# Earlier output norms and spills on another queue in a one-layer hybrid decoder kernel

## The chip, the cores and the metric

The kernel runs on one core of one Trainium2 chip. A core has TensorE (PE, the matrix multiplier; its weight loads are shown as PEld), VectorE (DVE), ScalarE (ACT), GpSimd (POOL) and SyncE (SP, which here only issues DMAs). Each engine works through its own list of instructions in order and waits for the others by semaphores. The metric is the device time of one execution in microseconds (us); lower is better.

## The reference, cut to what matters

One layer of a decoder for 256 prompt tokens and 8 sample tokens (264 in all). The parts that the change touches are the two mixers and the projection behind them:

```python
z = rmsnorm(x, g_mix) @ w_in
# recurrence ("rg"): gated linear recurrence over the prompt
h_rg, h_last = rglru(conv(z_rgx), r, i, lam, h0)
y_rg = rmsnorm(h_rg * gelu(z_rgg), g_rg_out)             # 1024 wide
# matrix memory ("ml"): 4 heads, q and k 128 wide, v 256 wide
num, den, C_new, n_new, m_new = mlstm(q, k, v, logi, logf, C0, n0, m0)
h_ml = rmsnorm(num / den, g_ml_out)                      # per head
y_ml = h_ml * sigmoid(z_o)
x = x + concat([y_rg, y_ml]) @ w_out
```

Behind them come cross attention over 256 memory tokens (w_q, w_k, w_v, w_o) and a gated feed-forward part. Outputs are the activations and the new states, the sample tokens' state matrices (o_sc, 4 heads of 8 tokens) among them.

## The kernel before, in words

**Tiling.** Activations lie transposed: 128 features on the partitions, 264 tokens along the free axis. The weights are worked off as a list `steps` of blocks of 2048 rows by 128 columns. A step is 16 chunks of 128 rows, and each chunk is three matmuls of 264 columns in fp32r (`mm3`: high by high, high by low, low by high, into one PSUM bank), so a step is 48 matmuls `mm<-B,W`. Steps 17 to 24 make v, 25 to 32 the recurrence's gate, 33 to 40 the output gate o, 41 to 56 w_out, and so on.

**Weights.** `load_piece` has SP load each block as two raw halves of 512 KB into 5 buffers, three steps ahead (a load waits until its buffer's old half has been split). `split_half`, a step ahead of use, has ACT copy a half to its high part and DVE subtract for the low part; `st["low"]` is that last subtraction.

**Side work.** Everything else is written as generators that are advanced between steps (`pump`); `yield STEP` puts the rest off to the next step. Small jobs that PE does in the middle of a step go through `later(job, after=k)`: jobs stand in one list, and after each chunk the first one's count falls by one, until at zero it is placed (`drip`); `finish` places everything at once. A step's evacuation (scaling the PSUM bank and so on) is kept in `pend` and written at the start of the next step, but not in steps 4, 5, 34 and 35 (L1439), so that the evacuations of steps 33, 34 and 35 are written at the start of step 36. SP's list is in the program's order; the other engines' lists are ordered by a scheduler within the program's dependences and priorities.

**The recurrence's output norm.** `rg_out` (L588) copies and subtracts the sum of squares `acc_rg` into two parts, waits a step, reduces over the partitions by two matmuls with `ones_r`, makes 1/sqrt by three Newton rounds on rows of 264 (`rstd_wide`, L384), and then scales each of the 8 blocks `h` and splits it in two (`split`) as `yrg`, which steps 41 onwards read chunk by chunk.

**The matrix memory.** For each head, `ml_heads` multiplies the masked weights with v, and writes k times its weights (`kw`) and, for every second head, v to DRAM (`kspill`, 128 KB a head, L774; `vspill`, 516 KB for two heads, L776); they are read back in the last 12 steps. The sample tokens' states are fetched by POOL: `B<-c0T` (L842, 512 KB) and two broadcast reads `B<-scr` (L846, 256 KB each) per half head, a half head ahead; ACT forms products `t<-B,B` from them, DVE updates the state, and POOL writes it out (`o_sc`, L870). POOL issues the spills in the same list. V's evacuation in that stage is `B<-ax 128x512` on ACT, which PE waits for with the head's product matmuls `ax<-B,B`.

**The matrix memory's norm.** `ml_norm` (L874) sums squares over partitions with `token_sums` (three matmuls `ax<-ones,B` a head, four heads), makes a factor `f` of 12 columns (4 heads by 3 windows of tokens) with a Newton chain on [128,12], spreads it over the partitions (`spread`, three fp32 matmuls a head: f's column, broadcast, against the identity), and multiplies `hh` by it. `evac_o` needs a head's scaled `hh`.

Of the kernel before, what the change touches and what calls it, by code (L numbers as in the profile page):

```python
# [10 lines left out]
F32 = mybir.dt.float32  # L11
F32R = mybir.dt.float32r
# [12 lines left out]
H = 4  # L25
# [65 lines left out]
def layer_kernel(ctx: ExitStack, tc, xT, memT, vec, wrg, w_in, w_out, w_q, w_k, w_v, w_o,  # L91
# [26 lines left out]
    def B(shape, dt=F32, skip=0):  # L118
        return view(sb.tile([P, SLOT], dt, tag="B", bufs=NB, name=nm("B")), shape, skip)
# [51 lines left out]
    steps = []  # L171
    LD, LS = 3, 1
    GATES = 8

    raws, splits = {}, {}

# [105 lines left out]
    def later(*fs, after=0):  # L282
        k = [after, list(fs)]
        drips.append(k)
        return k
# [13 lines left out]
    def bank(tag="mm"):  # L299
        return psm.tile([P, 512], F32, tag=tag, bufs=4, name=nm(tag))  # L300
# [58 lines left out]
    def spread(ps, c, n=N):  # L359

        for j in range(2 if n == T else 3):
            lo, hi = (j * P, j * P + P) if j < 2 else (T, N)
            i = pe.matmul(ps[:, lo:hi], c[j].to_broadcast([P, P]), ident[:, P - (hi - lo):], start=True, stop=True)
        return i
# [19 lines left out]
    def rstd_wide(acc, y, n):  # L384

        w = acc.shape[-1]
        hl, vt = B([P, 2, w], F32R), B([P, 3, w])
        act.activation(hl[:, 0], acc, AF.Copy)
        dve.tensor_sub(hl[:, 1], acc, hl[:, 0].bitcast(F32))
        yield STEP  # L390
        ps = bank("ax")
        for k in range(2):
            pe.matmul(ps[:, :w], ones_r, hl[:, k], start=k == 0, stop=k == 1)
        v, i, t = vt[:, 0], vt[:, 1].bitcast(I32), vt[:, 2]
        dve.tensor_scalar(v, ps[:, :w], 1.0 / n, EPS, op0=OP.mult, op1=OP.add)
        dve.tensor_single_scalar(i, v.bitcast(I32), 1, op=OP.logical_shift_right)
        dve.tensor_scalar(y.bitcast(I32), i, -1.0, 1597463007.0, op0=OP.mult, op1=OP.add)
        for _ in range(3):
            dve.tensor_mul(t, y, y)
            dve.scalar_tensor_tensor(t, t, -0.5, v, op0=OP.mult, op1=OP.mult)  # L400
            dve.scalar_tensor_tensor(y, t, 1.5, y, op0=OP.add, op1=OP.mult)
        yield 0.1

    def sumsq(acc, x, first):
        if first:
# [180 lines left out]
        return f  # L586

    def rg_out():  # L588
        yield STEP
        rr = ltmp()  # L590
        yield from rstd_wide(acc_rg, rr, RGB * P)
        st["yrg"] = HL(RGB)
        for n in range(RGB):
            h = rg["h"](n)
            dve.tensor_mul(h, h, rr)
            split(*st["yrg"](n), h, V("g_rg", n))
            yield 0.75

# [158 lines left out]
    def ml_heads():  # L757
        hT["t"] = Arr(8)
        hh = hT["t"]
        one = ones[:, 0:1]  # L760
        for h in range(H):
            while min(ml.get("pn", 0), ml.get("vtn", 0)) <= h:
                yield STEP
            while st["i"] < ml["pi", h] + 3:
                yield STEP
            vt = ml["vt", h]
            Pm, kw, p2 = ml["w", h]
            nps = bank("ax")
            for vb in range(2):
                o = vb * T  # L770
                pe.matmul(nps[:, o: o + T], vt[:, 0, vb * P: vb * P + P], Pm[:, 0:256], start=True, stop=False)
                pe.matmul(nps[:, o + P: o + T], vt[:, 1, vb * P: vb * P + P], Pm[:, 256:384],
                          start=False, stop=True)
            pool_e.dma_start(kspill[:, h, :], kw)  # L774
            if h % 2:
                pool_e.dma_start(vspill[h // 2], ml["vts"][h // 2].rearrange("p t h v -> p (t h v)"))  # L776
            dps = bank("ax")[:, 0:2]
            pe.matmul(dps[:, 0:1], Pm[:, 0:P], one, start=True, stop=True)
            pe.matmul(dps[:, 1:2], p2, one, start=True, stop=True)
            for vb in range(2):  # L780
                act.activation(hh(2 * h + vb)[:, 0:T], nps[:, vb * T: vb * T + T], AF.Copy)
            act.activation(den[:, 3 * h: 3 * h + 2], dps, AF.Abs)
        yield STEP
# [89 lines left out]
    def ml_norm():  # L873
# [15 lines left out]
        def sums(h):  # L889
# [10 lines left out]
                dve.tensor_mul(f, f, r)  # L900
            return i

        for h in range(H):
            k = later(lambda h=h: sums(h), after=3 if h else 1)
        while k[1]:
            yield STEP
        for h in range(H):
            ps = bank("ax")
            spread(ps, [f[:, 3 * h + j: 3 * h + j + 1] for j in range(3)])
            for vb in range(2):  # L910
                dve.tensor_mul(hh(2 * h + vb), hh(2 * h + vb), ps[:, :N])
            yield 0.7
            ml["nn"] = h + 1

    def evac_o(j):
        def f(ps):
# [512 lines left out]
    for i, (src, cols, pef, evf, need) in enumerate(steps):  # L1429
# [6 lines left out]
            if q in st:  # L1436
                finish(lambda: st[q].done)
        st["i"] = i
        if i not in (4, 5, 34, 35):  # L1439
            with tc.high_priority(300):  # L1440
                for e, x in pend:
                    e(x)
            pend = []
# [4 lines left out]
        if i + LS < len(steps) and steps[i + LS][1] > 1024:  # L1448
            split_half(i + LS, 1, parts)
        ps = pef(i)  # L1450
        if 1 <= i < 4:
            with tc.issue_after(st["split"].ins):
                for q in ((0, 1), (2,), (3,))[i - 1]:
                    square(q)
# [132 lines left out]
```

## Time and profile before

| quantity | value |
|---|---|
| time, median of 3 runs | 1537.24 us (1536.81 to 1538.69) |
| the profiled execution's own time | 1538.44 us |
| its span, first to last instruction | 1536.4 us (so 2.0 us lie around it) |
| granted TensorE clock, mean | 0.998 |
| busy: PE, DVE, ACT, POOL | 99%, 69%, 51%, 8% of the span |
| DMA rate over the span | 214 GB/s, 329 MB |

Times in the profile are in us from the span's start. A row of a timeline gives start, length, engine, line, operation, output<-input and the number of instructions put together; in square brackets stands idle time before it and what ended it. Nearly all instructions are recorded through one helper and so carry line L63; the names of tiles tell them apart. "L63 PE MATMUL mm<-B,W" is a weight matmul; "ax" is a PSUM bank of side work. Lengths of pipelined matmuls overlap, so the pitch from start to start is what counts. Some matmul records can be missing.

### The profile page before, as it was taken

How to read it: one execution, taken by the hardware profiler on the slowest of the kernel's cores; microseconds unless marked ns; L12 is line 12 of the kernel's file. 1: busy time of each engine (PE TensorE's matmuls, PEld its weight loads, DVE VectorE, ACT ScalarE, POOL GpSimd, SP SyncE). 2: the span in 40 equal slices, each digit the busy share in tenths (PEclk: the TensorE clock that was granted, in tenths of full speed). 3: DMA queues.
4: the chain of work that ended last, by engine and by line, in shares of the span. 5: the costliest groups of instructions: out<-in, count | busy, mean ns of one | idle time of the engine just before them, and what ended most of it. 6: DMA issues, size and time to landing. Idle time of an engine off the chain costs nothing.

```text
span 1536.4 us, 30014 instructions
## 1 busy us (share of the span) xinstructions
PE 1525.2 (99%) x12038; PEld 1490.6 (97%) x12038; DVE 1059.4 (69%) x2012; ACT 782.8 (51%) x1233; POOL 129.7 (8%) x195
## 2 busy tenths in 40 slices
PE   9999999999999999999999999999999999999997
PEld 9999999999998888899999999999999999999997
DVE  7976898878898989966665555455555544555554
ACT  7555784655555666654544444334444433344463
POOL 0001220000233434400000000000000000000000
PEclk9999999999999999999999999999999999999999
DMA  8646896556798798755555555555555555555573
GB/s 297 206 154 203 302 320 234 180 183 238 258 339 333 242 343 326 250 163 191 182 187 180 183 189 179 186 184 180 188 182 181 189 180 185 186 180 186 158 226 119
DMA packets 93659, 329.17 MB, mean 214 GB/s; under 512 B 10992, under 2 KB 11936, under 8 KB 93520
## 3 DMA queue, kind: packets, MB, share of 16 engines
q1 hardware_dynamic: 77904, 273.03, 53.1%
q0 software_dynamic: 15472, 54.22, 9.9%
q8 instruction: 94, 1.54, 0.4%
q14 instruction: 45, 0.37, 0.1%
q10 hardware_dynamic: 144, 0.01, 0.0%
HBM read 314.36 MB, written 12.86 MB: 213 GB/s over the span
## 4 chain that ended last, share of the span: by engine, by line
PE 95%; DMA 2%; ACT 1%; DVE 1%; issue 0%; POOL 0%; DVEq 0%; POOLq 0%
PE mm L63 91%; PE ax L63 4%; DMA B<-scr 1%; DMA xres<-xT 1%; DVE B L63 1%; DMA raw<-w_in 0%; ACT B L63 0%; DMA scr<-lt 0%; DMA vecs<-vec 0%; ACT t L63 0%; DVE W L63 0%; ACT L63 0%; ACT W L63 0%; POOL kspill L774 0%; DVE t L63 0%
## 5 line engine op out<-in xcount | busy, mean ns | idle before, releaser
L63 PE MATMUL mm<-B,W 128*128 128x264 f32 (+2 forms) x11008 | 1363.3, 285 | 0.6 <-DVE W L63 0.4
L63 PEld LDWEIGHTS mm<-B,W 128*128 128x128 f32 x11008 | 1340.5, 188 | 12.7 <-DVE W L63 0.6
L63 ACT ACTIVATE W<-raw 128x1024 fp32r<-128x1024 f32 (+2 forms) x520 | 536.6, 1034 | 637.3 <-PE mm L63 436.6
L63 DVE TENSOR_TENSOR W<-raw,W 128x1024 fp32r<-128x1024 f32 (+2 forms) x520 | 620.1, 1195 | 347.6 <-ACT W L63 346.4
L63 PE MATMUL mm<-W,B 128*128 128x512 f32 x384 | 92.4, 395 | 0.0
L63 PEld LDWEIGHTS mm<-W,B 128*128 128x128 f32 x384 | 70.9, 188 | 16.1
L1479 POOL TENSOR_TENSOR B<-B,rstd 128x264 f32<-128x264 f32 x4 | 2.8, 734 | 854.1 <-ACT rstd L63 854.1
L63 DVE TENSOR_TENSOR t<-mm,rstd 128x264 f32<-128x264 f32 x104 | 44.8, 432 | 43.5 <-PE mm L63 43.3
L63 DVE TENSOR_TENSOR xres<-xres,mm 128x264 f32<-128x264 f32 (+1 forms) x81 | 34.3, 425 | 34.5 <-PE mm L63 34.4
L63 DVE SCALAR_TENSOR_TENSOR B<-B,dw 128x256 f32<-128x256 f32 x128 | 53.9, 476 | 1.8 <-ACT dw L63 1.7
L63 DVE SCALAR_TENSOR_TENSOR dw<-B,qsm,dw 128x256 f32<-128x256 f32 x96 | 50.8, 538 | 1.9 <-ACT dw L63 1.6
L1115 POOL TENSOR_TENSOR dr<-dw,dr 128x256 fp32r<-128x256 f32 x32 | 38.5, 1205 | 102.6 <-ACT dr L63 102.5
L63 PE MATMUL ax<-B,B 128*128 128x256 f32 (+2 forms) x272 | 44.7, 303 | 1.0 <-ACT B L63 1.0
L63 PEld LDWEIGHTS ax<-B,B 128*128 128x128 f32 x272 | 38.4, 190 | 3.5 <-ACT B L63 1.2
L63 ACT ACTIVATE B<-xres,vecs 128x264 fp32r<-128x264 f32 (+1 forms) x64 | 31.0, 502 | 2.2 <-DMA xres<-xT 2.1
L1104 POOL DMA_DIRECT2D B<-kcT x32 | 17.4, 543 | 134.8 <-DVE B L63 126.5
L63 ACT ACTIVATE t<-t 128x264 f32<-128x264 f32 (+1 forms) x61 | 24.7, 407 | 4.5 <-DVE t L63 4.5
L63 ACT ACTIVATE dw<-B,qsm 128x256 f32<-128x256 f32 x32 | 16.3, 508 | 20.7 <-DVE B L63 9.2
L63 ACT ACTIVATE B<-t 128x264 fp32r<-128x264 f32 (+1 forms) x60 | 24.5, 408 | 4.4 <-DVE t L63 4.4
L63 ACT ACTIVATE t<-B,B 128x128 f32<-128x128 f32 x64 | 20.2, 388 | 12.1 <-DMA B<-scr 12.1
L63 ACT ACTIVATE t<-xres 128x264 f32<-128x264 f32 (+2 forms) x46 | 18.8, 410 | 14.6 <-DVE xres L63 14.6
L63 DVE SCALAR_TENSOR_TENSOR B<-xres,vecs,B 128x264 fp32r<-128x264 f32 x48 | 22.4, 490 | 1.1 <-ACT B L63 1.1
(168 smaller groups left out, 659.0 us busy)
## 6 DMA issues: line engine op xcount, KB each, us to landing
raw<-w_gu SPq DMA_DIRECT2D x176, 512.0 KB, 3.6
raw<-w_d SPq DMA_DIRECT2D x80, 512.0 KB, 3.6
raw<-w_in SPq DMA_DIRECT2D x78, 512.0 KB, 5.1
raw<-w_out SPq DMA_DIRECT2D x32, 512.0 KB, 3.6
raw<-w_q SPq DMA_DIRECT2D x32, 512.0 KB, 5.6
B<-kcT POOLq DMA_DIRECT2D x32, 512.0 KB, 8.0
B<-vcT POOLq DMA_DIRECT2D x32, 512.0 KB, 8.9
raw<-w_k SPq DMA_DIRECT2D x32, 512.0 KB, 6.3
```

What stands on the lines that cost most here:

```text
L63: return f(*a, **k)
L1104: pool_e.dma_start(kc, kcT[h, b])
L1115: pool_e.tensor_sub(wr[:, 1], acc, wr[:, 0].bitcast(F32))
L1479: e.tensor_mul(st["y"](c), st["y"](c), r)
```

## The change

Three things, each by moving or replacing instructions:

1. **Recurrence's output norm.** The wait of a step before the reduction is gone; its two matmuls are placed by `later(..., after=15)`. The scalings of the 8 blocks are tied to steps (`RGAT`) and to come behind that step's last weight subtraction.
2. **Matrix memory's norm.** The sums of the four heads follow each other by one chunk instead of three. The factor f (12 columns) is turned into rows once (`turn`: three fp32 matmuls with 4-column weights, output 4 rows of 264), split into high and low rows, and spread by two one-pass fp32r matmuls a head against a 4-row selector (`scale`), in place of three fp32 matmuls a head. The evacuations of steps 33 to 35 are now written at the end of step 36's code.
3. **Spills.** `kspill` and `vspill` are issued from SP's list instead of POOL's.

```diff
+    RGAT = (37, 37, 37, 38, 38, 38, 39, 39)
 def rstd_wide(acc, y, n):
-            pe.matmul(ps[:, :w], ones_r, hl[:, k], start=k == 0, stop=k == 1)
+            last = pe.matmul(ps[:, :w], ones_r, hl[:, k], start=k == 0, stop=k == 1)
...
-        yield 0.1
+        yield last
 def rg_out():
-        yield STEP
         rr = ltmp()
-        yield from rstd_wide(acc_rg, rr, RGB * P)
+        wide = rstd_wide(acc_rg, rr, RGB * P)
+        next(wide)
+        k = later(lambda: next(wide), after=15)
+        while k[1]:
+            yield STEP
         st["yrg"] = HL(RGB)
         for n in range(RGB):
+            while st["i"] < RGAT[n]:
+                yield STEP
             h = rg["h"](n)
-            dve.tensor_mul(h, h, rr)
+            with tc.issue_after(st["low"].ins):
+                dve.tensor_mul(h, h, rr)
             split(*st["yrg"](n), h, V("g_rg", n))
 def ml_heads():
-            pool_e.dma_start(kspill[:, h, :], kw)
+            sp.dma_start(kspill[:, h, :], kw)
             if h % 2:
-                pool_e.dma_start(vspill[h // 2], ml["vts"][h // 2].rearrange("p t h v -> p (t h v)"))
+                sp.dma_start(vspill[h // 2], ml["vts"][h // 2].rearrange("p t h v -> p (t h v)"))
 def ml_norm():
+        fp = bank("ax")
+        hl = B([P, 2, N], F32R)[0:4]
+        def turn():
+            fj = f.rearrange("p (h j) -> p j h", j=3)
+            for j, w0 in enumerate((0, P, T)):
+                w = min(P, N - w0)
+                i = pe.matmul(fp[0:4, w0: w0 + w], fj[:, j, :], ident[:, P - w:], start=True, stop=True)
+            act.activation(hl[:, 0], fp[0:4, :N], AF.Copy)
+            dve.tensor_sub(hl[:, 1], fp[0:4, :N], hl[:, 0].bitcast(F32))
+            return i
+        def scale(h):
+            ps = bank("ax")
+            sel = ident_r[:, h: h + 1].to_broadcast([4, P])
+            for k in range(2):
+                i = pe.matmul(ps[:, :N], sel, hl[:, k], start=k == 0, stop=k == 1)
+            with tc.issue_after(st["low"].ins):
+                for vb in range(2):
+                    dve.tensor_mul(hh(2 * h + vb), hh(2 * h + vb), ps[:, :N])
+            ml["nn"] = h + 1
+            return i
         for h in range(H):
-            k = later(lambda h=h: sums(h), after=3 if h else 1)
+            later(lambda h=h: sums(h), after=1)
+        for h in range(H):
+            if h == 0:
+                later(turn, after=19)
+            k = later(lambda h=h: scale(h), after=1 if h else 6)
         while k[1]:
             yield STEP
-        for h in range(H):
-            ps = bank("ax")
-            spread(ps, [f[:, 3 * h + j: 3 * h + j + 1] for j in range(3)])
-            for vb in range(2):
-                dve.tensor_mul(hh(2 * h + vb), hh(2 * h + vb), ps[:, :N])
-            yield 0.7
-            ml["nn"] = h + 1
 # the loop over the steps
-        if i not in (4, 5, 34, 35):
+        if i not in (4, 5, 34, 35, 36):
...
         ps = pef(i)
+        if i == 36:
+            with tc.high_priority(300):
+                for e, x in pend:
+                    e(x)
+            pend = []
```

What this does to the engines' lists shows in three places. Numbers behind a tile's name count the tiles; an `x2` is two equal instructions in a row.

**POOL's and SP's lists in steps 23 to 32.** POOL before, from the second half head's reads to the fourth's state: the spills stand between the state's writes and the next fetches.

```order
L846 DMA B_1957<-scr 128x512 x2
L776 DMA vspill<-B_1541 128x1032
L870 DMA o_sc<-B_1874 128x1024
L774 DMA kspill<-B_1862 128x256
L842 DMA B_2068<-c0T 128x1024
L846 DMA B_2069<-scr 128x512 x2
L870 DMA o_sc<-B_1956 128x1024
L774 DMA kspill<-B_1955 128x256
L774 DMA kspill<-B_2054 128x256
L774 DMA kspill<-B_2154 128x256
L842 DMA B_2262<-c0T 128x1024
```

POOL after, the same stretch:

```order
L853 DMA B_1957<-scr 128x512 x2
L877 DMA o_sc<-B_1874 128x1024
L849 DMA B_2068<-c0T 128x1024
L853 DMA B_2069<-scr 128x512 x2
L877 DMA o_sc<-B_1956 128x1024
L849 DMA B_2262<-c0T 128x1024
```

SP after, from the second load for step 29 to the first for step 32 (before, the same weight loads stand there with nothing between them):

```order
L188 DMA raw_2341<-w_in 128x1024
L781 DMA kspill<-B_1955 128x256
L783 DMA vspill<-B_1541 128x1032
L188 DMA raw_2448<-w_in 128x1024
L188 DMA raw_2450<-w_in 128x1024
L781 DMA kspill<-B_2054 128x256
L188 DMA raw_2557<-w_in 128x1024
L188 DMA raw_2559<-w_in 128x1024
L781 DMA kspill<-B_2154 128x256
L783 DMA vspill<-B_1542 128x1032
L188 DMA raw_2666<-w_in 128x1024
```

The six spills have left POOL, so that the fetch of B_2068 and B_2069 stands right behind the first state's write; on SP the first spill (not among these rows) stands behind the loads for step 28, and the last two stand between the loads for step 31 and those for step 32.

**ACT's list in step 24.** B_2069 holds what `scr` gives, W_2083 is the high part of half a weight block for step 25, and B_1542 is v, evacuated, for which PE waits. Before:

```order
L63 ACTIVATE B_1955<-B_1619,B_1955 128x128
L63 ACTIVATE W_2083<-raw_1938 128x8x128
L63 ACTIVATE t_2267<-B_2069,B_1545 128x128
L63 ACTIVATE B_1542<-ax_2055 128x2x256
L63 ACTIVATE t_2267<-B_2069,B_1545 128x128
L63 ACTIVATE t_2273<-B_2069,B_1545 128x128 x2
L63 ACTIVATE B_2054<-B_2054 128x384
```

After:

```order
L63 ACTIVATE B_1955<-B_1619,B_1955 128x128
L63 ACTIVATE t_2267<-B_2069,B_1545 128x128 x2
L63 ACTIVATE t_2273<-B_2069,B_1545 128x128 x2
L63 ACTIVATE W_2083<-raw_1938 128x8x128
L63 ACTIVATE B_1542<-ax_2055 128x2x256
L63 ACTIVATE B_2054<-B_2054 128x384
```

All four products from B_2069 now stand ahead of the weight copy and of v's evacuation; before, one of them did.

**PE's list around step 37.** c_3089 and c_3109 are the factor f, B_3111 its rows in two parts, mm_3326 (before) and mm_3318 (after) the bank of step 37, mm_3208 (after) that of step 36. Before, the spreads stand five matmuls into step 37:

```order
L63 MATMUL mm_3326<-B_144,W_3244 128x264 x2
L63 MATMUL mm_3326<-B_145,W_3244 128x264
L63 MATMUL ax_3185<-ident,c_3089 128x128 x2
L63 MATMUL ax_3185<-ident,c_3089 128x8
L63 MATMUL ax_3191<-ident,c_3089 128x128 x2
L63 MATMUL ax_3191<-ident,c_3089 128x8
L63 MATMUL ax_3197<-ident,c_3089 128x128 x2
L63 MATMUL ax_3197<-ident,c_3089 128x8
L63 MATMUL ax_3203<-ident,c_3089 128x128 x2
L63 MATMUL ax_3203<-ident,c_3089 128x8
L63 MATMUL mm_3326<-B_144,W_3244 128x264 x2
```

After, the turn stands three quarters into step 36, and the selector matmuls between steps 36 and 37:

```order
L63 MATMUL mm_3208<-B_173,W_3115 128x264
L63 MATMUL ax_3110<-ident,c_3109 4x128 x2
L63 MATMUL ax_3110<-ident,c_3109 4x8
L63 MATMUL mm_3208<-B_183,W_3115 128x264
L63 MATMUL mm_3208<-B_184,W_3115 128x264
```

```order
L63 MATMUL mm_3208<-B_183,W_3115 128x264
L63 MATMUL ax_3265<-B_3111,ident_r 128x264
L63 MATMUL ax_3270<-B_3111,ident_r 128x264
L63 MATMUL ax_3275<-B_3111,ident_r 128x264
L63 MATMUL ax_3280<-B_3111,ident_r 128x264
L63 MATMUL ax_3275<-B_3111,ident_r 128x264
L63 MATMUL ax_3270<-B_3111,ident_r 128x264
L63 MATMUL ax_3265<-B_3111,ident_r 128x264
L63 MATMUL ax_3280<-B_3111,ident_r 128x264
L63 MATMUL mm_3318<-B_144,W_3202 128x264
```

Twelve fp32 matmuls are replaced by three fp32 and eight fp32r ones. The two `ax<-B,ones_r` matmuls of the recurrence's norm, which stood in the middle of step 37, stand after the last matmul of step 34.

## The prediction

> **What bounds the kernel now.** I read the page first: busy shares, clock, and the chain of work that ended last.
>
> ```profile
> PE 1525.2 (99%) x12038; PEld 1490.6 (97%) x12038; DVE 1059.4 (69%) x2012; ACT 782.8 (51%) x1233; POOL 129.7 (8%) x195
> PE 95%; DMA 2%; ACT 1%; DVE 1%; issue 0%; POOL 0%; DVEq 0%; POOLq 0%
> ```
>
> TensorE is busy for 99% of the span and makes 95% of the chain; its granted clock is 0.998, so it isn't slowed. Time can then go in two ways only: PE has fewer or shorter instructions, or one of its waits goes. What the waits hold in all is the next view, PE's waits by releaser (us in total, times, longest):
>
> ```profile
> PE ax L63 <- ACT B L63: 1.5, 2, 1.0
> PE mm L63 <- DVE ones L63: 1.1, 1, 1.1
> PE mm L63 <- DVE W L63: 0.4, 1, 0.4
> PE mm L63 <- ACT W L63: 0.2, 1, 0.2
> ```
>
> About 3.2 us, of which 1.1 is the start (`ones`). So the waits that a reordering could take away are worth about 2 us. The third view gives the price of PE's work: the groups of PE by form (busy us, mean ns).
>
> ```profile
> L63 PE MATMUL mm<-B,W 128*128 128x264 f32 x10496 | 1269.9, 282 | 0.6 <-DVE W L63 0.4 <-ACT W L63 0.2
> L63 PE MATMUL ax<-ident,c 128*128 128x128 f32 x32 | 5.2, 288 | 0.0
> L63 PE MATMUL ax<-B,ident_r 4*128 4x256 f32 x8 | 2.0, 328 | 0.0
> ```
>
> 1269.9 us over 10,496 weight matmuls are 0.121 us each (the 282 ns are latency, which overlaps). A step of 48 is 5.8 us. Now PE's timeline where the norms lie (start, length, count):
>
> ```profile
> 234.69 0.72 PE L63 MATMUL ax<-ones,B 128*128 128x1 f32 x6
> ...
> 241.63 7.30 PE L63 MATMUL mm<-B,W 128*128 128x264 f32 x59
> 248.77 2.74 PE L63 MATMUL ax<-ident,c 128*128 128x128 f32 x24
> 251.37 2.55 PE L63 MATMUL mm<-B,W 128*128 128x264 f32 x19
> 253.75 0.41 PE L63 MATMUL ax<-B,ones_r 128*128 128x264 f32 x2
> 254.00 22.07 PE L63 MATMUL mm<-B,W 128*128 128x264 f32 x183
> 276.50 8.72 PE L63 MATMUL mm<-B,W 128*128 128x264 f32 x70 [0.43 <-DVE W L63]
> ```
>
> The reader sees the first of four sums, the spread of the matrix memory's factor (24 passes, since each fp32 matmul is two), the reduction of the recurrence's norm, and one wait 0.43 long at 276, in step 41. It is booked to a weight split, but the recurrence's scaled blocks are what comes last there:
>
> ```profile
> 273.61 1.70 DVE L63 SCALAR_TENSOR_TENSOR B<-B,vecs,B 128x264 fp32r<-128x264 f32 x4
> 275.23 1.22 DVE L63 TENSOR_TENSOR W<-raw,W 128x1024 fp32r<-128x1024 f32 x1
> 276.36 0.89 DVE L63 SCALAR_TENSOR_TENSOR B<-B,vecs,B 128x264 fp32r<-128x264 f32 x2
> ```
>
> DVE makes the low parts of `yrg` (B<-B,vecs,B) until 275.2, and a weight subtraction then ends about when PE goes on; step 41 is where `yrg` is read first.
>
> **The change, part by part.**
>
> *The matrix memory's spread.* Removed: the 24 passes, which hold PE from 248.77 to 251.37, 2.60 us; the 19 weight matmuls behind them take 2.38 to the next group, 0.10 over their 19 at 0.120, which goes with them. Saved 2.70. Added, `turn`: a quarter of that work with 4-column weights. Its price isn't in the trace; a quarter of 2.60 is 0.65, with the way back 0.75; 0.70 is taken. Added, `scale`: eight one-pass matmuls of 264 columns whose weights have 4 rows. The nearest rows are the pairs against `ident_r` with 4 rows, ahead of step 24:
>
> ```profile
> 159.24 0.50 PE L63 MATMUL ax<-B,ident_r 4*128 4x256 f32 x2
> 159.67 0.92 PE L63 MATMUL ax<-B,B 128*128 128x256 f32 x4
> 160.43 0.60 PE L63 MATMUL ax<-ident,B 128*128 128x128 f32 x4
> ```
>
> The pair takes 0.43 to the next group, where two at 0.117 (256 of 264 columns at 0.121) would take 0.23: 0.20 over for entering. The four behind take 0.76 for 0.47: up to 0.29 over for leaving, though part of that is the next group's own change of form. Eight in a row enter and leave once: 8 x 0.121 = 0.97, plus 0.20 to 0.49; 0.35 is taken, so 1.32. The Trainium skill, "TensorE: Matmul & The Clock Gate", section "Why this matters for your kernels", says that a single matmul with K = 32 takes as long as one with K = 128; by it these eight cost 0.97 and the whole sum would be 2.7 saved instead of 2.3. The rows above show more than that, and the rows decide. The four sums only move (one chunk apart instead of three), so PE's count there stays. In all: -2.70 + 0.70 + 1.32 = **-0.68**, with ends at -0.5 and -1.1.
>
> What this could bring instead: the chain of sums, Newton, turn, ACT copy, DVE subtraction, selectors must be done in time. The sums stand earlier and closer than before; of the Newton chain the trace shows the end.
>
> ```profile
> 245.94 0.17 DVE L63 TENSOR_TENSOR c<-c,c 128x12 f32<-128x12 f32 x1
> ```
>
> f is done at 246.1 now, from a last sum that ends at 241.6. Of the 59 matmuls from 241.63 the last 53 are step 36 and five of step 37, so step 36 begins at 248.77 - 53 x 0.121 = 242.4, and PE reaches the turn 36 matmuls later, at 246.7: 0.6 to spare even if the chain ended no sooner than now, and its last sum is earlier. The copy and the subtraction behind the turn (an estimate of 0.43 each, from DVE's 1.70 for four operations of 264 columns above) have the 12 matmuls that follow it, 1.4 us. Behind the selectors only the weights of step 37 are queued, and for the scaled `hh` waits only `evac_o`, on DVE and ACT. I cost this at nothing; if f is late, PE stands still until it is there, up to 0.5 us.
>
> *The recurrence's norm.* Reduction and Newton rounds move ahead by more than two steps, and the scalings to steps 37 to 39, so that a whole step of 5.8 us lies between the last of them and step 41's reads. That is the room that DVE's other work there may use up. The `ones_r` pair costs the same 0.25 (253.75 to 254.00) elsewhere. They stand at the start of step 35, six matmuls (0.7) ahead of the first sum at 234.69, so at 234.0, and need DVE's subtraction from `acc_rg`:
>
> ```profile
> 233.34 0.43 DVE L63 TENSOR_TENSOR B<-acc_rg,B 128x264 fp32r<-128x264 f32 x1
> ```
>
> It ends at 233.8: tight, by 0.2. The wait at 276 goes. Its worth: 254.00 to 276.50 is 22.50 us for 183 matmuls, 0.54 over 183 at 0.120, while records can be missing from the row (then less); the listed idle time is 0.43, and the next matmul is longer too. I take **-0.60**, bounds 0.43 and 0.75. What is late next there: the weight split ending at 276.4, if it doesn't move up with DVE's freed time; three of the recurrence's operations stood ahead of it, so it does.
>
> *The spills.* The second large wait on PE is at the start of step 25:
>
> ```profile
> 166.71 0.50 PE L63 MATMUL ax<-B,ident_r 4*128 4x256 f32 x2
> 168.20 0.92 PE L63 MATMUL ax<-B,B 128*128 128x256 f32 x4 [0.99 <-ACT B L63]
> 163.78 1.05 ACT L63 ACTIVATE W<-raw 128x1024 fp32r<-128x1024 f32 x1
> 167.26 0.40 ACT L63 ACTIVATE t<-B,B 128x128 f32<-128x128 f32 x1 [2.44 <-DMA B<-scr]
> 167.57 0.58 ACT L63 ACTIVATE B<-ax 128x512 f32<-128x512 f32 x1
> ```
>
> The same pair needed 0.43 ahead of step 24 and needs 1.49 here: 1.06 lost. PE waits for v's evacuation on ACT (167.57), which stands behind a product whose input, `B<-scr`, lands at 167.24. Why so late, POOL's timeline shows:
>
> ```profile
> 156.28 0.54 POOL L776 DMA_DIRECT2D vspill<-B  x1 [7.73 <-ACT B L63]
> 156.81 0.54 POOL L870 DMA_DIRECT2D o_sc<-B  x1
> 157.80 0.54 POOL L774 DMA_DIRECT2D kspill<-B  x1 [0.45 <-ACT B L63]
> 158.34 0.53 POOL L842 DMA_DIRECT2D B<-c0T  x1
> 158.86 1.08 POOL L846 DMA_DIRECT2D B<-scr  x2
> 150.00:160.00 10.00, 10.00 (x78) 9.37 (x77) 7.05 (x29) 8.77 (x23) 3.21 (x6) 1.00 0.78 279
> 160.00:170.00 10.00, 9.01 (x71) 8.59 (x70) 9.98 (x36) 6.63 (x14) 1.09 (x2) 1.00 0.96 294
> ```
>
> (The last two rows are windows: busy of PE, PEld, DVE, ACT, POOL, clock, DMA share, GB/s.) POOL stood 7.73 us behind the `vspill` for which ACT wasn't ready, then behind `kspill`. Without the spills `o_sc` can go when DVE has written its state:
>
> ```profile
> 154.86 0.48 DVE L63 SCALAR_TENSOR_TENSOR B<-B,bcs,t 128x256 f32<-128x256 f32 x1
> ```
>
> That is 155.35, so c0T follows at 155.9 and the first `scr` read at 156.4, 2.4 us sooner, with 0.66 MB (516 KB and 128 KB) less ahead of it, 2.2 us at 294 GB/s. It took 8.38 us (158.86 to 167.24); it lands at 164.8 if it still takes that, and at 162.6 if the bytes ahead count in full. But ACT's order has changed against it: four products (4 x 0.31), the weight copy (1.05) and only then the evacuation (0.58), 2.87 us from the landing L to PE, where it was 0.96. PE is free at 166.71 + 0.43 = 167.14, so there is no wait if L is 164.3 or less, and as long a wait as before at 165.3. Between 162.6 and 164.8 the wait is 0 to 0.5: I take **-1.06**, the whole of it, with -0.6 as the other end.
>
> On SP the spills only write what has long been ready, so nothing queued behind them waits for ACT; an issue costs SP a few tenths. But they are transfers ahead of weights. The tight place is step 32, since the last 0.66 MB stand right ahead of its first half, which ACT already awaits today:
>
> ```profile
> 211.43 1.06 ACT L63 ACTIVATE W<-raw 128x1024 fp32r<-128x1024 f32 x1 [0.20 <-DMA raw<-w_in]
> 216.37 5.79 PE L63 MATMUL mm<-B,W 128*128 128x264 f32 x47
> ```
>
> The half lands at 211.4, copy and subtraction need 1.06 and 1.22, and PE reads the block from 216.7 (the last three of step 31 open this row): slack about 2.7 us with the work between. I cost it at nothing: the same bytes went through the same engines before, only sooner or later in this stage.
>
> **Sum.** -0.68 - 0.60 - 1.06 = -2.3. The profiled execution, 1538.44 (its span 1536.4 and 2.0 around it), would be 1536.1, its span 1534.1; it lies 1.2 above the median of the runs, 1537.24, from which 2.3 leaves **1534.9**. 0.2%, about what a measurement of this kernel can tell from no change, is 3.07 us: the likeliest result is under it.
>
> **The rivals.**
>
> *The wait at step 25 stays.* The fetch issues sooner but L is near 165.3, because the DMA engines are slower to serve it than before: -0.68 - 0.60 = -1.3, 1535.9. For it: the DMA share is 0.96 from 160 to 170. Against: 0.78 before, where the read now starts. This is also the case in which the third part doesn't do what it says.
>
> *Slower: ACT stuck behind the products.* If L doesn't move at all from 167.24 (say the read is served behind the weights that SP issues between), PE goes on 2.87 later, at 170.1, and loses 3.0 instead of 1.06: +1.9 - 0.68 - 0.60 = +0.6, 1537.8. It decides from L = 166.6, where the sum is nought. Against: 2.4 us of sooner issue.
>
> *Weights behind spills.* At half of 294 GB/s, the other half going to POOL's transfers, the 0.66 MB hold the first half of step 32 for 4.5 us, over the slack of 2.7 by 1.8; 0.5 is saved, 1536.7. Against: half of the bytes may go while SP waits for a buffer anyway, which leaves it within the slack. The Trainium skill, "DMA: Bandwidth & Descriptors", section "Queues, rings and completion order", says that a DMA engine goes round the queue rows packet by packet; by it a spill on POOL's row shares turns with the weights, and one on SP's row stands ahead of them. No row of this trace shows a weight load behind a spill in one queue.
>
> *Norms late.* The two tight places (the subtraction at 233.8, f at the turn) miss by 0.3 to 0.5 each: 1535.6.
>
> **How the numbers follow.** Forecast 0.5; wait at step 25 stays 0.2; weights behind spills 0.14; norms late 0.08; slower by ACT 0.08. The range goes down to 1533.6, where the ends of the terms add up (-1.1 - 0.75 - 1.06 = -2.9) and 0.7 is left for the runs' own scatter of 1536.81 to 1538.69; up to 1536.9 it takes in all but the last rival. Faster by over 0.2%: 0.20, the low end of the forecast with that scatter. Slower by over 0.2%: 0.05, the slow rival with scatter or a worse L. Within: 0.75.
>
> **What would show it.** Right: eight `ax<-B,ident_r` matmuls in 1.3 us before step 37; no idle time in step 41; `B<-scr` landing under 164.4 and no wait on ACT at step 25; POOL without a gap of 7.7 us. Wrong: a PE wait of over 1 us at step 25 or 32, or at a selector; or a time under 1533.6, which would mean PE work that I haven't found.

## The result, and the profile after

The changed kernel takes 1535.95 us (median of 17 runs, 1535.52 to 1538.10) against 1538.38 us (17 runs, 1536.81 to 1543.12) for the kernel before, run beside it: ratio 0.9983, 95% interval 0.9976 to 0.9989, 2.4 to 2.6 us faster and, at 0.17%, just under the 0.2% that the prediction named as hard to tell from no change; the interval reaches past it. The profiled execution took 1535.74 us with a span of 1534.0, against 1538.44 and 1536.4. On record stood 1534.9 us, or a span of 1534.1. The span was met; the median lies 1.05 us above the forecast, since the kernel before, from whose 1537.24 the forecast was worked out, has a median of 1538.38 in the 17 runs.

First the chain of the kernel after, by engine and by tile, then its waits of PE by releaser (us in total, times, longest):

```profile
PE 99%; DVE 0%; DMA 0%; ACT 0%; DVEq 0%; issue 0%; ACTq 0%
PE mm L63 94%; PE ax L63 5%; DVE B L63 0%; DMA raw<-w_in 0%; ACT W L63 0%; ACT B L63 0%; DVEq L1596 0%; ACTq L63 0%
```

```profile
PE mm L63 <- DVE ones L63: 1.1, 1, 1.1
PE ax L63 <- ACT B L63: 0.4, 1, 0.4
```

Both of the waits that the prediction spoke of are gone. `DMA B<-scr`, which had 1% of the chain, is gone from it too. PE's timeline of the kernel after, ahead of step 25, and then ACT's and POOL's in the same stretch:

```profile
166.81 0.50 PE L63 MATMUL ax<-B,ident_r 4*128 4x256 f32 x2
167.24 0.92 PE L63 MATMUL ax<-B,B 128*128 128x256 f32 x4
```

```profile
163.51 1.27 ACT L63 ACTIVATE t<-B,B 128x128 f32<-128x128 f32 x4
164.68 1.05 ACT L63 ACTIVATE W<-raw 128x1024 fp32r<-128x1024 f32 x1
165.63 0.57 ACT L63 ACTIVATE B<-ax 128x512 f32<-128x512 f32 x1
```

```profile
154.57 0.54 POOL L877 DMA_DIRECT2D o_sc<-B  x1 [6.07 <-DVE t L63]
155.10 0.53 POOL L849 DMA_DIRECT2D B<-c0T  x1
155.62 1.07 POOL L853 DMA_DIRECT2D B<-scr  x2
```

POOL now stands behind DVE's state alone, and the read issues at 155.62 instead of 158.86. It lands at 161.98 (the trace's DMA record), so all four products have their input when ACT comes to them at 163.51; v's evacuation ends at 166.20, and the pair takes its 0.43 again.

PE's timeline of the kernel after, around the norms:

```profile
233.00 0.40 PE L63 MATMUL ax<-B,ones_r 128*128 128x264 f32 x2
...
238.72 7.43 PE L63 MATMUL mm<-B,W 128*128 128x264 f32 x60
246.09 0.64 PE L63 MATMUL ax<-ident,c 128*4 128x128 f32 x6
246.65 1.73 PE L63 MATMUL mm<-B,W 128*128 128x264 f32 x12
248.32 1.22 PE L63 MATMUL ax<-B,ident_r 4*128 4x264 f32 x8
249.47 35.75 PE L63 MATMUL mm<-B,W 128*128 128x264 f32 x296
```

There is the turn (0.56 to the next row), the eight selector matmuls (1.15), and 296 weight matmuls from step 37 on without a wait in step 41. Counted out by the trace's single matmuls, the starts of the steps differ from those of before by +0.10 from step 6 to step 24 (the start of the kernel), -0.97 from step 25, -0.75 at step 36, -1.55 from step 38 and -2.29 from step 42 on. So the three parts are worth 1.06 us at step 25, 0.55 at the spread (0.80 between steps 36 and 38, of which 0.25 is the `ones_r` pair that was only moved) and 0.74 in step 41, 2.35 in all.

### The profile page after: what moved, and what is told of

Same layout as the page of the kernel before. It is cut to its first block, busy times and chain, and to the rows that moved or that the text cites. A ratio compares the mean times of both kernels' runs of the same rounds, so it can differ in the third digit from the quotient of the medians.

```text
span 1534.0 us, 29990 instructions
## 1 busy us (share of the span) xinstructions
PE 1524.8 (99%) x12028; PEld 1490.9 (97%) x12028; DVE 1059.3 (69%) x2013; ACT 784.0 (51%) x1234; POOL 126.1 (8%) x189
## 4 chain that ended last, share of the span: by engine, by line
PE 99%; DVE 0%; DMA 0%; ACT 0%; DVEq 0%; issue 0%; ACTq 0%
PE mm L63 94%; PE ax L63 5%; DVE B L63 0%; DMA raw<-w_in 0%; ACT W L63 0%; ACT B L63 0%; DVEq L1596 0%; ACTq L63 0%
```

## The experiments

Ratios are to the kernel before, with 95% intervals. The position of a step is read as above, from the start of its first matmul against the kernel before.

### Each part alone, and one part undone

Spills back in POOL's list, all else as changed:

```diff
-            sp.dma_start(kspill[:, h, :], kw)
+            pool_e.dma_start(kspill[:, h, :], kw)
-                sp.dma_start(vspill[h // 2], ...)
+                pool_e.dma_start(vspill[h // 2], ...)
```

> The changed kernel with the six spills back in POOL's list; both norms as changed. Theory (three independent parts; the spills in POOL's in-order list hold the fetch back, and v's evacuation on ACT stands behind a product of that fetch): PE's wait ahead of step 25 is back at 1.06 us, the read of scr lands near 167, steps 26 to 34 start where they did before, and the span is 1.0 to 1.1 above the changed kernel, 1.3 us under before (ratio 0.9991). Rival (the norms' part made the difference and the spills only share in it): under 0.3 us of wait ahead of step 25, span within 0.4 of the changed kernel.

Measured: ratio 0.9988 (0.9979 to 0.9996), 12 runs, median 1537.37: 1.2 us under before, as the theory has it. The profiled execution, though, had another fault: PE lost 3.1 us ahead of step 24 (2.5 of it listed as waits), and did not wait ahead of step 25, since PE itself was late there. That wait is taken up below. The times agree with the theory's size within their interval (0.6 to 3.2 us under before); the expected trace was not seen in this execution, in which the read landed at 170.42.

The kernel before with only the spills moved (the same two lines the other way round):

> The kernel before with only the spills issued from SP's list. Theory: the wait ahead of step 25 goes, step 26 starts 1.0 us sooner, the wait in step 41 stays (0.4 to 0.7), and the span falls by 1.0 to 1.1 (ratio 0.9993). Rival (weights queue behind the spills on SP): the first half of step 32 lands later than 211.4 less the shift and PE waits there, up to 1.8 us; span 0.5 or less under before, or above it.

Measured: ratio 0.9987 (0.9979 to 0.9996), span 1535.2. Step 25 starts 1.06 sooner relative to step 24; nothing waits in step 32; the wait in step 41 is still there. PE's timeline of this kernel:

```profile
275.47 9.80 PE L63 MATMUL mm<-B,W 128*128 128x264 f32 x79 [0.43 <-DVE W L63]
```

The theory holds; weights behind spills cost PE nothing in this profile.

The kernel before with only the recurrence's norm changed (`rstd_wide`, `rg_out` and `RGAT` of the change):

> The kernel before with only the recurrence's norm changed (no step of waiting, reduction after the last matmul of step 34, scalings tied to steps 37 to 39). Theory: PE's work is unchanged and the wait in step 41 goes: step 42 starts 0.6 to 0.75 sooner, span -0.6 to -0.75 (ratio 0.9996). Rival (the wait moves to a weight split that DVE makes late because the scalings now stand behind st[low] of steps 37 to 39): waits of 0.3 or more on DVE in steps 38 to 40, span within 0.3 of before.

Measured: ratio 0.9993 (0.9984 to 1.0003), so the time can't tell it from before. The trace can: step 42 starts 0.73 sooner relative to step 41, and the wait there is gone. PE's timeline of this kernel has one row from step 37 through step 41, with no idle time in it:

```profile
252.24 33.02 PE L63 MATMUL mm<-B,W 128*128 128x264 f32 x273
```

The moved wait of the rival isn't seen. (This execution also had no wait ahead of step 25, with the read landing at 165.69: with the spills on POOL that wait comes and goes.)

The kernel before with only the matrix memory's norm changed (`ml_norm` and the loop's `36`):

> The kernel before with only the matrix memory's norm changed (closer sums, turn, selectors, evacuations of steps 33 to 35 at the end of step 36). Theory: the spread's 2.7 us are replaced by 2.1 us, so PE starts step 38 0.55 sooner; the wait in step 41 stays, since the recurrence's scalings are where they were: span -0.4 to -0.6 (ratio 0.9997). Rival (the wait in step 41 came from DVE's load by the old norm's multiplications, not from the recurrence's own place): the wait goes as well, span -1.2 to -1.3.

Measured: ratio 1.0052 (1.0038 to 1.0067), 8 us slower (6 runs). Both expectations fell. PE's waits, then ACT's timeline of this kernel:

```profile
PE ax L63 <- ACT B L63: 9.2, 3, 7.0
```

```profile
254.40 0.92 ACT L63 ACTIVATE B<-B,vecs 128x264 fp32r<-128x264 f32 x2 [2.27 <-DVE B L63]
256.46 0.92 ACT L63 ACTIVATE B<-B,vecs 128x264 fp32r<-128x264 f32 x2 [1.14 <-DVE B L63]
257.29 0.36 ACT L63 ACTIVATE B<-ax 4x264 fp32r<-4x264 f32 x1
```

The copy of the factor's rows (`B<-ax 4x264`), which the selectors need, stands in ACT's list behind the split copies of the recurrence, and these wait for DVE's scalings. PE stands still 7.0 us at the selectors. So the first two parts aren't independent: the new matrix-memory norm needs the recurrence's scalings out of its way. The wait in step 41 is gone here too, but PE comes to that step 10.7 us later than before, so this says nothing on its cause. And since PE waits at the selectors here, no run shows the new spread alone: its 0.55 us are read from the step starts of the changed kernel, where the 0.80 between steps 36 and 38 come back within 0.01 in four further profiles that keep both norms and the 4-row selectors as changed.

### What the ties do

The changed kernel without the ties:

```diff
-            while st["i"] < RGAT[n]:
-                yield STEP
-            with tc.issue_after(st["low"].ins):
-                dve.tensor_mul(h, h, rr)
+            dve.tensor_mul(h, h, rr)
```

> The changed kernel without the ties of the recurrence's scalings (neither to steps 37 to 39 nor behind the last weight subtraction). Theory (the scalings only have to be done before step 41): no wait in step 41, span within 0.2 of the changed kernel. Rival (the ties keep DVE free for the matrix memory's factor and the weight splits): DVE makes the scalings in steps 35 and 36, the factor's Newton chain or a weight split comes late, and PE waits at the turn, at the selectors or in step 36 or 37 by 0.3 to 2 us.

Measured: ratio 1.0043 (1.0031 to 1.0056). PE's timeline, DVE's, and the windows (PE, PEld, DVE, ACT, POOL busy, clock, DMA share, GB/s) of this kernel:

```profile
252.16 1.05 PE L63 MATMUL ax<-ident,c 128*4 128x128 f32 x6 [5.77 <-DVE c L63]
253.14 3.01 PE L63 MATMUL mm<-B,W 128*128 128x264 f32 x12
```

```profile
242.47 0.16 DVE L63 TENSOR_TENSOR c<-c 128x12 f32<-128x12 f32 x1
242.55 2.49 DVE L63 TENSOR_TENSOR B<-B,lt 128x264 f32<-128x264 f32 x7
244.95 0.17 DVE L63 SCALAR_TENSOR_TENSOR c<-c,c 128x12 f32<-128x12 f32 x1
245.03 1.22 DVE L63 TENSOR_TENSOR W<-raw,W 128x1024 fp32r<-128x1024 f32 x1
246.17 1.70 DVE L63 SCALAR_TENSOR_TENSOR B<-B,vecs,B 128x264 fp32r<-128x264 f32 x4
247.79 0.16 DVE L63 SCALAR_TENSOR_TENSOR c<-c,c 128x12 f32<-128x12 f32 x1
```

```profile
248.00:252.00 4.00, 0.00 (x0) 0.00 (x0) 3.79 (x12) 0.00 (x0) 0.00 (x0) 0.65 0.48 166
252.00:256.00 4.00, 3.84 (x18) 3.33 (x18) 0.43 (x2) 0.38 (x1) 0.00 (x0) 0.50 0.14 53
```

The factor's Newton operations (`c<-c`, 0.17 each) are threaded one by one between the scalings and splits (0.35 to 0.43 each) in DVE's list, and the factor is done at 252.0 instead of 245.4. PE pays more than the wait: its granted clock is 0.65 in the window that lies inside the wait and 0.50 in the next (the two window rows), and the 12 matmuls that took 1.67 to the next row take 2.94. From 238.96 to 257.24 in place of 238.72 to 249.47, the stretch is 7.5 us longer, 5.8 of it wait. No wait came in step 41, so for that wait the earlier place of the norm is enough without the ties. The rival was right in place and far too small in size.

Ties to the steps alone:

```diff
-            with tc.issue_after(st["low"].ins):
-                dve.tensor_mul(h, h, rr)
+            dve.tensor_mul(h, h, rr)
```

> The changed kernel with the recurrence's scalings tied to steps 37 to 39 but no longer behind the step's last weight subtraction. In DVE's list the eight multiplications then stand among the factor's Newton operations again. Theory (what cost PE 5.8 us without both ties is DVE's in-order list, in which the factor's short operations stand behind the scalings): eight multiplications of 0.35 are 2.8 us, less the 0.6 that the factor has to spare, so PE waits about 2 us at the turn, plus up to 1 us of lower clock; span 2 to 3.2 above the changed kernel. Rival (the step numbers alone protect the factor): no wait at the turn, span within 0.2.

Measured: ratio 1.0010 (0.9999 to 1.0021), 12 runs, median 1540.89; a wait of 2.9 us at the turn (about 2 was expected), and the clock stays at 1.00 behind it in the profiled execution. DVE's timeline, then PE's, of this kernel:

```profile
243.33 0.16 DVE L63 TENSOR_TENSOR c<-c 128x12 f32<-128x12 f32 x1
243.41 2.49 DVE L63 TENSOR_TENSOR B<-B,lt 128x264 f32<-128x264 f32 x7
245.81 0.17 DVE L63 SCALAR_TENSOR_TENSOR c<-c,c 128x12 f32<-128x12 f32 x1
```

```profile
249.79 0.63 PE L63 MATMUL ax<-ident,c 128*4 128x128 f32 x6 [2.88 <-DVE c L63]
```

In the changed kernel that `c<-c,c` starts 0.20 us behind the `c<-c`, here 2.48. The wait is longer than expected because one more weight subtraction (1.22) also stands ahead of the factor's last operations. The median is 4.8 us above the changed kernel's 1536.10 beside it, more than the 2 to 3.2 that were expected: the profiled execution, 1539.72, is among the shorter ones, and the three longest, 1543.17 to 1544.74, have a mean granted clock of 0.995 or 0.996 where it has 0.998. What they lost it on was not profiled. The step numbers alone don't protect the factor; the tie behind the weight subtraction does, since it puts the eight multiplications behind the Newton operations in DVE's list.

### What held the read back, and who waited for it

Spills in POOL's list, but each issued only behind the next fetch's reads:

```diff
-            sp.dma_start(kspill[:, h, :], kw)
+            spills.append((kspill[:, h, :], kw))
...
                     ahead = fetch(n // 2, n % 2)
+                    if n >= 2:
+                        flush(cn["read"])   # pool_e.dma_start of each, tied behind the read
```

> The changed kernel with the spills in POOL's list, but tied behind the reads of the half head that is fetched next, so that no fetch stands behind a spill that isn't ready. Theory (the place in POOL's in-order list was the harm, not POOL's issuing): the third half head's read lands near 162 to 163, no wait ahead of step 25, span within 0.2 of the changed kernel. Rival (spills issued by POOL delay the fetches wherever they stand, by their bytes): the read lands at 165 or later, and PE waits 0.5 us or more ahead of step 25, or in steps 26 to 33.

Measured: the read issues at 156.08 and lands at 162.10, no wait ahead of step 25, span 1533.9, ratio 0.9987 (0.9978 to 0.9997). The place of the spills in POOL's list was the harm; that POOL issues them, and not SP, shows no cost in this trace (the medians, 1536.73 and 1536.10 for the changed kernel beside it, have intervals that overlap).

Spills on POOL where they were, and v's evacuation tied ahead of the products of that read on ACT:

```diff
+                        with tc.issue_after(ml["ev", 2].ins) if (h, b4) == (1, 0) else ExitStack():
-                        act.activation(t2[:, vb, :], ...)
+                            act.activation(t2[:, vb, :], ...)
```

> The changed kernel with the spills back in POOL's list, and on ACT v's evacuation tied ahead of the products from the late read. The read still lands near 167. Theory (PE waits for the evacuation alone, and that only because it stands behind a product in ACT's list): the wait ahead of step 25 goes though the read is as late as before; span within 0.2 of the changed kernel. Rival (the late transfer itself holds the stage up): ACT then stands before the products and makes the weight copies for step 26 late, PE waits 0.5 us or more in step 26 or 27, and the span is 0.5 to 1.1 above the changed kernel.

Measured: the read lands as late as 168.44, yet step 25 starts 1.06 sooner relative to step 24 than before. ACT's timeline of this kernel:

```profile
165.78 0.58 ACT L63 ACTIVATE B<-ax 128x512 f32<-128x512 f32 x1
168.47 1.29 ACT L63 ACTIVATE t<-B,B 128x128 f32<-128x128 f32 x4 [2.11 <-DMA B<-scr]
```

The evacuation is out 2.1 us before the late read lands, and no later step pays for it. The times don't show the gain: ratio 0.9992 (0.9983 to 1.0001), median 1537.11, and the span of 1535.3 is 1.3 above the changed kernel's. In the profiled execution 0.66 us of that is a wait ahead of step 24 again, and 0.27 stands ahead of step 6.

### The price of the selectors

Selectors over all 128 rows, the rows of the factor in four of them and zeros in the rest:

```diff
-        hl = B([P, 2, N], F32R)[0:4]
+        hf = B([P, 2, N], F32R)
+        pool_e.memset(hf.bitcast(F32), 0.0)
+        hl = hf[0:4]
-            sel = ident_r[:, h: h + 1].to_broadcast([4, P])
+            sel = ident_f[:, h: h + 1].to_broadcast([P, P])   # identity's columns, 128 rows
```

> The changed kernel with the selectors over all 128 rows: the weights are columns of the identity 128 rows deep, the rows of the factor stand in the first 4 of 128 rows and the others are zero (POOL clears them ahead). The same eight matmuls, the same result. Theory (what the eight cost over 8 x 0.121 = 0.97 is the change from weights of 128 rows to weights of 4 rows and back): the eight take 0.97 to 1.0 with the way back instead of 1.25, span 0.2 to 0.3 under the changed kernel. Rival (the number of rows doesn't matter, what costs is the change of operand): the same 1.15 to the next group and 0.1 behind it, span unchanged. Second risk: clearing the rows on POOL delays the turn; then a wait of PE at the selectors.

Measured, in PE's timeline of this kernel:

```profile
247.07 1.73 PE L63 MATMUL mm<-B,W 128*128 128x264 f32 x12
248.64 1.13 PE L63 MATMUL ax<-B,ident_f 128*128 128x264 f32 x8
249.61 12.63 PE L63 MATMUL mm<-B,W 128*128 128x264 f32 x104
```

The eight take 0.97, which is 0.121 each, and from the row behind the turn to step 37 it is 2.54 instead of 2.82. That 0.28 is not all: in the changed kernel the first weight matmul behind the selectors is slow as well, and from step 36 to step 38 this kernel needs 0.37 less. By the trace's single matmuls of the changed kernel, the last weight matmul ahead takes 0.21 to the next start, the first selector 0.22, the last 0.21 and the first weight matmul behind 0.23, where the matmuls within a group take about 0.12. So the price is about 0.2 on the way to 4 rows and 0.2 on the way back. Ratio 0.9986 (0.9977 to 0.9994): such a step can't be read from times.

One matmul of 128 rows behind each head's pair (its result isn't read):

```diff
+            with tc.issue_after(i.ins):
+                i = ml["sep"] = pe.matmul(ps[:, 384:512], ones_r, ones_r, start=True, stop=True)
```

> The changed kernel with the selectors head by head, and behind each head's pair one more matmul of 128 columns with 128-row weights, whose result nobody reads. Theory (each change between 4-row and 128-row weights costs 0.1 each way beside the matmul): four more matmuls at 0.06 are 0.24, and three more pairs of changes are 0.55 to 0.6, so step 37 starts 0.8 later than in the changed kernel. Rival (only a matmul's columns count): 0.24 later.

Measured, in PE's timeline and the windows of this kernel:

```profile
248.53 0.50 PE L63 MATMUL ax<-B,ident_r 4*128 4x264 f32 x2
248.96 0.33 PE L63 MATMUL ax<-ones_r 128*128 128x128 f32 x1
249.22 0.51 PE L63 MATMUL ax<-B,ident_r 4*128 4x264 f32 x2
```

```profile
252.00:256.00 4.00, 4.00 (x23) 4.00 (x22) 4.00 (x10) 0.10 (x1) 0.00 (x0) 0.57 0.36 135
```

A pair and its separator take 0.69, where the columns alone would be 0.30: 0.39 for each change to 4 rows and back, more than the 0.2 expected and close to the 0.37 above. Step 37 starts 1.5 later than in the changed kernel by that. Unexpected is the window row: the clock falls to 0.57 right behind, without a listed wait. For about 3.3 us, from 252.4, the single weight matmuls stand 0.220 us apart instead of 0.121, and step 37 takes 1.5 us longer. Its single time, 1538.94, can't be set beside medians.

### The wait ahead of step 24, and the version that removes it

The changed kernel once more:

> The changed kernel itself once more, beside the next three on the same chip. Theory (the first read of scr lands between 150 and 154 by chance in any kernel, and PE waits ahead of step 24 when it lands later than about 151.2): the same step starts as in its first profile within 0.1 from step 4 to 59, except for such a wait; ratio to before 0.998 to 0.9989. Rival (the first profile was a lucky one in other places too): new waits at step 25, 32 or 36 to 41.

Measured: ratio 0.9983 (0.9975 to 0.9992), 12 runs from 1535.33 to 1539.86. The profiled execution was the longest of them, with a span of 1538.1. ACT's timeline, then PE's, of this execution:

```profile
154.05 2.46 ACT L63 ACTIVATE t<-B,B 128x128 f32<-128x128 f32 x8 [8.24 <-DMA B<-scr]
156.53 1.28 ACT L63 ACT_TABLE_LOAD   x1
157.82 0.53 ACT L63 ACTIVATE B<-B 128x384 f32<-128x384 f32 x1
```

```profile
160.10 0.92 PE L63 MATMUL ax<-B,B 128*128 128x256 f32 x4 [0.44 <-DVE B L63]
163.18 1.11 PE L63 MATMUL ax<-ident,B 128*128 128x128 f32 x4 [2.16 <-DVE B L63]
163.95 7.07 PE L63 MATMUL mm<-B,W 128*128 128x264 f32 x48
```

The first read of `scr` landed at 154.03 here and at 150.93 in the first profile. ACT's exponential for the first head stands behind its products; PE waited 2.6 us, and the next 48 matmuls took 7.07 instead of 6.00 at a lower clock (0.86 and 0.71 in the windows 160:164 and 164:168). In all else the steps kept their distances. Over all profiles of the study, landings of 150.2 to 151.4 went with a loss of 0 to 0.8 us ahead of step 24, 152.2 and 152.7 with 0.7 and 1.0, 154.0 and 154.1 with 3.3 and 3.1. POOL issues this read at 145.8 to 147.8, ahead of every spill, and the two norms come more than 75 us later, so neither the spills nor the norms stand ahead of it; what makes it land late stays open. The kernel before scatters more, with 12 of 33 runs over 1540 on this chip and none of the 12 runs here; it has one profile, so what its long runs hold is not known.

On ACT, the products of the first read tied behind the first head's work and those of the third behind v's evacuation, with the 128-row selectors (`ml["ex", 0]` is the second scaled copy of k for head 0, `ml["ev", 2]` v's evacuation for head 2):

```diff
+                        tie = ml["ex", 0] if (h, b4) == (0, 0) else ml["ev", 2] if (h, b4) == (1, 0) else None
+                        with tc.issue_after(tie.ins) if tie else ExitStack():
-                        act.activation(t2[:, vb, :], ...)
+                            act.activation(t2[:, vb, :], ...)
```

> The changed kernel with the 128-row selectors, and on ACT the products of the first read tied behind the first head's work (exponential, v's evacuation, two scaled copies of k), and those of the third read behind v's evacuation. Theory (PE's chance waits ahead of step 24 come from that work standing behind the products of a late read in ACT's list): no wait ahead of steps 24 and 25 whenever the read lands, 0.3 us less at the selectors, and less scatter; ratio to before 0.9975 to 0.998. Rival (the products then come so late that the states, and the fetches behind them, are late): PE waits 0.5 us or more in steps 25 to 34, ratio 0.9985 or above.

Measured: ratio 0.9977 (0.9967 to 0.9986), 9 runs from 1534.70 to 1536.15, median 1535.64. The 0.37 us at the selectors are there again. In its profile the third read landed at 166.13 and PE waited neither ahead of step 24 nor of step 25. The interval overlaps that of the changed kernel (median 1536.10 beside it), so it isn't shown to be faster in the median. None of the 9 runs is over 1536.2, where the changed kernel had 3 of 12 over 1537.4. That its first read landed at 151.0 in the profiled execution leaves one thing open: the tie at step 24 wasn't seen at work in a trace with a late read.

## Why the prediction was right, point by point

**The bound.** PE's work and its few waits were the only places where time could go, and all of the difference was found there. That the sum came out so near, 2.35 against 2.34, is partly luck: the spread brought 0.13 less than forecast and step 41 0.14 more.

**The spread.** Forecast 0.68, measured 0.55. The term that was mis-sized is the added work: by the step starts the turn and the selectors with their changes of form cost 2.15 (2.70 less 0.55), where 2.02 was put. By the single matmuls the turn makes 0.76 of it, where 0.70 was put (0.57 for its six passes, and 0.2 for entering and leaving), and the selectors 1.35, where 1.32 was put. The price for the changes that the rows gave (0.35) was near: 0.37 went when the selectors were over 128 rows. The Trainium skill, "TensorE: Matmul & The Clock Gate", section "Why this matters for your kernels", has a matmul over 32 rows take the same time as one over 128; within a run of 4-row matmuls the trace agrees (0.12 each), but passing from 128-row weights to 4-row ones and back is dearer.

**Step 41.** Forecast 0.60, measured 0.74, at the upper bound. That the recurrence's part alone removes it, and that it stays when only the spills are moved, shows the cause.

**Step 25.** Forecast 1.06, measured 1.06. The read issued at 155.62 instead of the 156.4 that were worked out, and landed at 161.98, a little ahead of 162.6 to 164.8. Two kernels separate the links: behind POOL's fetch order (spills later in the same list) the wait goes, and behind ACT's order (evacuation first) it goes although the read is late. The prediction took the single wait of one execution as the whole effect; with the spills on POOL the wait was 0.6 in one further profile (the matrix memory's norm alone) and absent in another (the recurrence's norm alone). The fastest runs of the two kernels lie only 1.3 to 1.4 us apart (1536.81 and 1535.52; 1536.70 and 1535.33), about the 1.29 of the other two parts; that fits a wait which the fastest runs of before don't have, but none of those runs was profiled. In the times the part alone is worth 1.3 us by medians, with an interval of 0.6 to 3.2.

**Step 32.** No wait came. The first half landed at 208.9 and ACT waited for it with time in hand: of its 13.9 us in the queue (12.9 before) the spills may have made one, but it was issued 3.6 us sooner. So the rival of weights behind spills is refuted for this place. That an issue costs SP a few tenths held for the weight loads (0.33 us in the trace) and not for the spills: the six took SP 0.45 to 1.77 us each, the two ahead of this load 1.77 and 1.62, and no wait of PE came of it.

**The norms in time.** The tight place at the start of step 35 wasn't tight: the subtraction from `acc_rg` ended at 230.4, not 233.8, and the pair started at 233.0. The factor was done at 245.36 and the turn at 246.09, 0.7 to spare (0.6 forecast).

**What failed in it** is not a number of the sum but what was costed at nothing. "If f is late, up to 0.5 us" was priced for this exact order alone. The prediction treated the ties of the scalings as details of the second part and never priced the order without them: they hold off a wait of 2.9 (one tie gone) or 5.8 us (both), more than the whole gain. And it summed three parts as independent, when the matrix memory's part alone is 8 us slower.

## What to carry to other kernels

Where engines work through lists in order, look for short operations that stand behind long ones of another chain: tying the long ones behind a later landmark was worth more here (2.9 and 5.8 us of waits held off) than the work that was saved. Keep what waits for a transfer behind what the busiest engine waits for, on the queue that issues as much as on the engine that computes. Before splitting a change into parts, ask which part clears the way for the other.

## What the runs showed of the hardware that was not expected

PE's granted clock falls after some waits, and a wait then costs more than its length: with a wait of 5.8 us it was 0.65 in the window of 4 us inside the wait and 0.50 in the next; behind 2.2 us (after 0.4 shortly ahead) 48 matmuls took 7.07 instead of 6.00; behind a single wait of 2.9 us it stayed at 1.00; and behind four 0.69-us groups of selectors with separators, with no wait listed, it fell to 0.57. The Trainium skill, "TensorE: Matmul & The Clock Gate", section "What's actually happening", says that the clock is halved or full by the activity in a free-running window of about 3.4 us; such a window agrees with the 2.9 us being free in one run and the shorter 2.6 in another not, and with the 3.3 us in which matmuls stood 0.220 apart instead of 0.121. The kernel without a listed wait shows that the clock can fall without one; that the thin work of the selector groups did it is likely, but not shown.

A change between weights of 128 rows and of 4 rows costs PE 0.37 to 0.39 us for the way there and back, beside the matmuls themselves. About half of it lies in the last matmul ahead of a change, so a timeline row that starts with the 4-row group doesn't show all of it.
